# A state-space mixer's sample states: loads, multiplies and stores written in other places, the SiLUs queued behind an exponential, and the state stores issued from GpSimd's queue

## The chip, the cores and the metric

The kernel runs on one core of a Trainium2 chip. The metric is the device time of one execution in microseconds (us). The core has five engines with instruction queues of their own: TensorE (PE in the profile), VectorE (DVE), ScalarE (ACT), GpSimd (POOL) and SyncE (SP). Each queue runs in order; semaphores tie them together. SP computes nothing here and issues transfers (DMAs).

## The reference, cut to what matters

One inference step of a two-layer network for a prompt of 512 positions and 8 samples of 8 positions (64 more columns), with d_model 1024. Layer 0 is a convolution and attention mixer, layer 1 a Mamba-2 mixer with 32 heads of 64 channels, a state of 128 and 4 groups of 8 heads; each is followed by a convolutional feed-forward block. The change is in layer 1's mixer. What it computes for the 8 samples, whose states come in as `state_ssm` and go out as `ssm_s` (the prompt's last state goes out as `ssm_p`), is this:

```python
def step(hc, inp):                     # ssd_scan: the prompt in 4 chunks of 128, a sample in one of 8
    dec, st = inp
    return dec[..., None, None] * hc + st, hc
h_final, h_prev = lax.scan(step, h0, (chunk_decay, states))
y_off = jnp.einsum('bclgn,bcgrpn,bclgr->bclgrp', cc, h_prev, jnp.exp(acum))
y = (y_diag + y_off).reshape(b, t, h, p)
...
y = (y + d_skip[:, None] * xs).reshape(b, t, D_INNER) * jax.nn.silu(z)
y = rmsnorm(y.reshape(b, t, SSM_GROUPS, gs), gn_g).reshape(b, t, D_INNER)
return y @ w_out, new_conv, new_ssm
```

So each sample's old state is read by a product with C (`y_off`), multiplied by a decay, added to the sample's new part and stored.

## The kernel before, in words

All activations stay in the core's memory, channels in partitions, with 576 columns (512 prompt, 64 sample) taken in two halves of 288. A large projection is done as three matmuls for each 128 x 128 block of weights, because values are split in a high and a low part: lines 160, 161 and 162, tile `mm`, with `wh`/`wl` the weights' parts (made by ACT, line 150, and DVE, line 151) and `hh`/`hl` or `yh`/`yl` the activations'. These matmuls are most of the kernel's work.

The second mixer, `mix1`, goes over 4 groups g of 8 heads. `ssd(g)` is a Python generator that emits the group's scan in pieces; `run` puts pieces of projection work (the z projection of the group, `z_units`, and the output projection of the group before, `out_tile`) between them. `gate(g)` then multiplies by silu(z), normalises and splits the result. The Python order is not the order that runs: a scheduler, at build time, writes each engine's queue from it with the dependences and costs that it assumes. `keep_in_program_order(m)` makes the next matmul stay behind m on TensorE, and `issue_after(i)` makes what is written in it stay behind instruction i on i's engine.

Steps and names of `ssd(g)`:

- `hst` (lines 983 to 1000): the prompt's states at the ends of 4 chunks; the last is stored to `ssm_p` by SP (line 1000).
- `carried(t)` for t = 0..3: a load `ea2`, an exponential, the product `py` (line 1034).
- `decays(r)`, two for each t: SP loads `acb` (line 1017), ACT makes four ReLUs and an exponential of it (lines 1021, 1022), DVE multiplies it (line 1023).
- `outputs(t)`: eight matmuls `yp` (line 1047) that read the two `acb`; DVE adds them to `xs`.
- `samples(bh)`, after t = 1 and after t = 3: for four samples, SP loads their old states `h0` (line 1060; the profile cuts digits from names and calls it `h`), TensorE makes `pyo` from them (line 1064, four matmuls into four strips of 32 rows), DVE `yo` from it (line 1066), TensorE the new part `pst` (line 1071), GpSimd multiplies `h0` by the decay `cds` (line 1072), DVE adds `pst` (line 1075), SP stores it to `ssm_s` (line 1076).
- `ysp` (lines 1095, 1100): the samples' outputs, with a product that reads `yo`.

All of `xs`, `acb`, `h0`, `hst`, `zs`, `yh`/`yl` and others come from one list of 48 + 9 equal slots (`S`, `NSLOT`, `EXTRA`), first freed, first reused. A load into a slot waits until its last user is done, a store's landing included. GpSimd also sets and copies the borders of the convolution's buffers (`cbuf`, lines 789 to 798) for the next group's projections, and SP loads all weights.

Of the kernel before, what the change touches and what calls it, by code (L numbers as in the profile page):

```python
# [14 lines left out]
P = 128  # L15
NP = 512
# [34 lines left out]
class Builder:  # L51
    NSLOT = 48
    EXTRA = 9
# [721 lines left out]
    def mix1(self):  # L775
# [60 lines left out]
        v = self.Z("sp_v", W, bufs=1)  # L836
# [6 lines left out]
        e, z, z2, q = (self.Z(n_, W, bufs=1) for n_ in ("sp_e", "sp_z", "sp_z2", "sp_q"))  # L843
# [16 lines left out]
        nc.scalar.activation(ea, self.pv("alog", 0, 32), AF.Exp, bias=zero)  # L860
        da = self.Z("da", W, bufs=1)
# [52 lines left out]
        def ssd(g):  # L914
# [85 lines left out]
            nc.sync.dma_start(d["ssm_p"][g], H[3])  # L1000
# [13 lines left out]
            def decays(r):  # L1014

                acb = self.S("acb", NP)
                nc.sync.dma_start(acb, acd[8 * g + r, 0:NP].partition_broadcast(P))
                for c in range(4):
                    cs = slice(c * P, (c + 1) * P)
                    o = c * 32 + 8 * g + r  # L1020
                    nc.scalar.activation(acb[:, cs], acb[:, cs], AF.Relu, bias=ac[:, o:o + 1], scale=-1.0)  # L1021
                nc.scalar.activation(acb, acb, AF.Exp, scale=-1.0)
                nc.vector.tensor_tensor(acb, acb, cbm[:, :NP], op=MUL)
                return acb
# [14 lines left out]
            def outputs(t, ea2, pair):  # L1039

                yp = self.ps("yp", "yp")
                for c in range(4):
                    cs = slice(c * P, (c + 1) * P)
                    for hh in (1, 0):
                        r = 2 * t + hh
                        rows, ch = slice(hh * 64, hh * 64 + 64), slice(r * 64, r * 64 + 64)
                        m = nc.tensor.matmul(yp[rows, cs], xdt[c][:, ch], pair[hh][:, cs], start=True, stop=True)  # L1047
                        if c or not hh:
                            self.tc.keep_in_program_order(m)
                x = xs[t][:, :NP]  # L1050
                nc.vector.scalar_tensor_tensor(x, x, self.pv("dsk", 4 * g + t), yp, op0=MUL, op1=ADD)
                nc.vector.tensor_tensor(x[:, P:], x[:, P:], ea2, op=ADD)
                self.free(pair, ea2)

            def samples(bh):

                h0 = []
                for b4 in range(4):
                    h0.append(self.S("h0", NP))
                    nc.sync.dma_start(h0[-1], d["h0"][4 * bh + b4, g])  # L1060
                pyo = self.ps("pyo", "pyo")
                for b4 in range(4):
                    b = 4 * bh + b4
                    nc.tensor.matmul(pyo[b4 * 32:b4 * 32 + 32, :], cf[:, NP + 8 * b:NP + 8 * b + 32], h0[b4], start=True, stop=True)  # L1064
                o = self.S("yo", NP)
                nc.vector.tensor_tensor(hp(o), hp(pyo), eax[:, bh * 32 + 8 * g:bh * 32 + 8 * g + 8].unsqueeze(2).broadcast_to([P, 8, 64]), op=MUL)
                yo.append(o)
                for b4 in range(4):
                    b = 4 * bh + b4
                    pst = self.ps("pst")  # L1070
                    nc.tensor.matmul(pst, b3[bh][:, b4 * P:(b4 + 1) * P], x3[bh], start=True, stop=True)
                    nc.gpsimd.tensor_tensor(hp(h0[b4]), hp(h0[b4]),  # L1072
                                            cds[:, b * 32 + 8 * g:b * 32 + 8 * g + 8].unsqueeze(2).broadcast_to([P, 8, 64]),
                                            op=MUL)
                    nc.vector.tensor_tensor(h0[b4], h0[b4], pst, op=ADD)
                    nc.sync.dma_start(d["ssm_s"][b, g], h0[b4])
                    self.free(h0[b4])
                    if b4 % 2:
                        yield

            for t in range(4):
                ea2 = carried(t)
                pair = []
                for hh in range(2):
                    pair.append(decays(2 * t + hh))
                    yield
                outputs(t, ea2, pair)
                yield
                if t % 2:
                    yield from samples(t // 2)  # L1090
# [15 lines left out]
        def z_units(g):  # L1106
            zss[g] = [self.S("zs") for _ in range(4)]

            def evac(t):
                return lambda half, p: nc.scalar.activation(zss[g][t][:, HALF[half]], p[:, :HB], AF.Copy)  # L1110
            return [(d["w_in_o"][4 * g + t], P, evac(t)) for t in range(4)]

        def gate(g, yv):
# [4 lines left out]
            for t in range(4):  # L1118
                nc.scalar.activation(zs[t], zs[t], AF.Silu)
# [26 lines left out]
        for g in range(4):  # L1146
# [3 lines left out]
            if g:  # L1150
# [19 lines left out]
            if g:  # L1170
                self.free(prev)
# [180 lines left out]
```

## Time and profile before

| | |
|---|---|
| median of 3 runs | 1595.83 us (1595.36 to 1596.58) |
| the profiled execution | 1596.65 us, of which 1594.9 us is the span from the first to the last instruction |
| TensorE busy | 1560.2 us (98%) |
| VectorE, ScalarE, GpSimd busy | 999.7, 656.1, 149.4 us |
| mixer 1, from its norm to the start of the next block | about 676 to 1150 us of the span |

Times in the views are microseconds from the start of the span. A matmul's record gives its own duration, but TensorE is pipelined, so the next matmul starts before it ends: what a matmul costs on the path is the distance from its start to the next start. A row that groups matmuls counts records; one matmul with 512 columns of 32-bit data leaves two records (x2). In brackets behind a row stands how long the engine sat idle before it, and what ended that. "A <- B" in the list of waits reads: A waited for B.

### The profile page before, as it was taken

Reading aid. Unit: us, or ns where it says so; the run is one execution under the profiler, and the core shown is the slowest. Engines: PE = TensorE matmul, PEld = TensorE weight load, DVE = VectorE, ACT = ScalarE, POOL = GpSimd, SP = SyncE. Lnnn points to the kernel's source line nnn. Section 1 sums busy time; section 2 is a strip of 40 time slices with the busy share of each in tenths; the row PEclk is TensorE's granted clock in tenths of the full one; section 3 lists DMA queues with packets and bytes.
Section 4 is the critical chain, followed back from the end, with each engine's and each line's share of the span. In section 5 each row is a group of like instructions: output and inputs, shape, how many; then the busy total and the mean of one; then the engine's idle time right before and its main releaser. Section 6 shows DMA issues by size and latency. Waiting matters only on the chain.

```text
span 1594.9 us, 28738 instructions
## 1 busy us (share of the span) xinstructions
PE 1560.2 (98%) x11709; PEld 1479.2 (93%) x11709; DVE 999.7 (63%) x1750; ACT 656.1 (41%) x1210; POOL 149.4 (9%) x362
## 2 busy tenths in 40 slices
PE   8999999999999999999999999999999999999999
PEld 8976799999999999998987987998899999999999
DVE  7958486663564464678885686676776643663552
ACT  6257363321232222479654655556443221221220
POOL 0026001000000000101202101101110000000000
PEclk9999999999999999999999999999999999999999
DMA  7514223222222222226245226235222232223222
GB/s 229 117 54 102 70 83 101 80 81 92 80 77 84 93 80 75 74 82 203 74 120 186 74 81 195 89 96 182 81 89 84 80 91 83 80 73 97 83 82 76
DMA packets 69841, 157.60 MB, mean 99 GB/s; under 512 B 20158, under 2 KB 24510, under 8 KB 69710
## 3 DMA queue, kind: packets, MB, share of 16 engines
q1 hardware_dynamic: 69710, 155.77, 31.9%
q8 instruction: 92, 1.51, 0.4%
q14 instruction: 39, 0.32, 0.1%
HBM read 140.54 MB, written 15.21 MB: 98 GB/s over the span
## 4 chain that ended last, share of the span: by engine, by line
PE 82%; DVE 7%; ACT 4%; DMA 4%; issue 1%; POOL 1%; SPq 0%; ACTq 0%; DVEq 0%; POOLq 0%
PE mm L160 24%; PE mm L161 24%; PE mm L162 24%; DMA acb<-acd 2%; DVE cconv L801 1%; PE mm L559 1%; PE yp L1047 1%; DMA h<-in_h 1%; PE pyo L1064 1%; PE pt L182 1%; DVE ca L436 1%; ACT wh L150 1%; DVE wl L151 1%; ACT acb L1021 1%; PE pr L193 1%
## 5 line engine op out<-in xcount | busy, mean ns | idle before, releaser
L160 PE MATMUL mm<-hh,wh 128*128 128x288 f32 (+1 forms) x2288 | 682.8, 299 | 8.4 <-ACT wh L150 7.7
L161 PE MATMUL mm<-hl,wh 128*128 128x288 f32 (+1 forms) x2288 | 678.6, 297 | 0.0
L162 PE MATMUL mm<-hh,wl 128*128 128x288 f32 x2288 | 677.6, 296 | 0.0
L150 ACT ACTIVATE wh<-wr 128x1024 fp32r<-128x1024 f32 (+1 forms) x215 | 223.4, 1039 | 541.0 <-PE mm L161 273.6
L160 PEld LDWEIGHTS mm<-hh,wh 128*128 128x128 f32 (+1 forms) x2288 | 429.8, 188 | 14.9 <-ACT wh L150 7.9
L161 PEld LDWEIGHTS mm<-hl,wh 128*128 128x128 f32 (+1 forms) x2288 | 430.2, 188 | 5.6 <-issue 3.8
L162 PEld LDWEIGHTS mm<-hh,wl 128*128 128x128 f32 x2288 | 430.7, 188 | 2.7 <-issue 1.3
L151 DVE TENSOR_TENSOR wl<-wr,wh 128x1024 fp32r<-128x1024 f32 (+1 forms) x215 | 259.2, 1206 | 77.5 <-ACT wh L150 77.3
L160 PE MATMUL mm<-yh,wh 128*128 128x288 f32 x960 | 286.8, 300 | 2.2 <-ACT yh L170 2.2
L161 PE MATMUL mm<-yl,wh 128*128 128x288 f32 x960 | 288.2, 300 | 0.1
L162 PE MATMUL mm<-yh,wl 128*128 128x288 f32 x960 | 284.8, 297 | 1.4 <-DVE wl L151 1.4
L162 PEld LDWEIGHTS mm<-yh,wl 128*128 128x128 f32 x960 | 181.6, 189 | 6.1 <-issue 4.1
L161 PEld LDWEIGHTS mm<-yl,wh 128*128 128x128 f32 x960 | 181.9, 189 | 5.3 <-issue 4.0
L160 PEld LDWEIGHTS mm<-yh,wh 128*128 128x128 f32 x960 | 181.5, 189 | 4.4 <-ACT yh L170 2.6
L259 DVE TENSOR_TENSOR x<-x,mm 128x288 f32<-128x288 f32 x192 | 85.4, 450 | 157.4 <-PE mm L162 157.2
L304 DVE TENSOR_TENSOR gbuf<-mm,rs 128x224 f32<-128x224 f32 x44 | 17.2, 391 | 108.0 <-PE mm L162 108.0
L315 ACT ACTIVATE gsilu<-gconv,par 128x512 f32<-128x512 f32 x44 | 31.8, 723 | 115.5 <-DVE gconv L312 115.5
L312 DVE SCALAR_TENSOR_TENSOR gconv<-gbuf,par,gconv 128x592 f32<-128x592 f32 x88 | 73.1, 831 | 1.5
L325 DVE TENSOR_TENSOR gsilu<-mm,gsilu 128x288 f32<-128x288 f32 x88 | 40.0, 454 | 49.7 <-PE mm L162 49.7
L801 DVE SCALAR_TENSOR_TENSOR cconv<-cbuf,par,cconv 128x600 f32<-128x600 f32 x72 | 61.5, 857 | 13.0 <-ACT cconv L799 12.0
L307 POOL COPY fpo<-gbuf 128x2 f32<-128x2 f32 x44 | 12.4, 281 | 497.6 <-DVE gbuf L304 497.6
L1072 POOL TENSOR_TENSOR h<-h,cds 128x512 f32<-128x512 f32 x32 | 36.7, 1166 | 186.5 <-PE pyo L1064 167.8
(306 smaller groups left out, 1640.9 us busy)
## 6 DMA issues: line engine op xcount, KB each, us to landing
wr<-in_w_gate SPq DMA_DIRECT2D x44, 512.0 KB, 3.3
wr<-in_w_up SPq DMA_DIRECT2D x44, 512.0 KB, 3.3
wr<-in_w_in_o SPq DMA_DIRECT2D x40, 512.0 KB, 3.5
wr<-in_w_down SPq DMA_DIRECT2D x32, 448.0 KB, 3.4
wr<-in_w_down SPq DMA_DIRECT2D x16, 512.0 KB, 3.5
acb<-acd SPq DMA_DIRECT2D x32, 256.0 KB, 3.9
h<-in_h SPq DMA_DIRECT2D x32, 256.0 KB, 3.5
out_ssm_s<-h SPq DMA_DIRECT2D x32, 256.0 KB, 2.1
```

Source lines behind the costliest of these rows:

```text
L150: nc.scalar.activation(hi[:, :n], raw[:, :n], AF.Copy)
L151: nc.vector.tensor_tensor(lo[:, :n], raw[:, :n], hi[:, :n].bitcast(F32), op=SUB)
L160: nc.tensor.matmul(out, hi[:, ws], xh[:, sl], start=i == 0, stop=False)
L161: nc.tensor.matmul(out, hi[:, ws], xl[:, sl], start=False, stop=False)
L162: nc.tensor.matmul(out, lo[:, ws], xh[:, sl], start=False, stop=i == n - 1)
L259: nc.vector.tensor_tensor(self.x[m][:, sl], self.x[m][:, sl], p[:, :HB], op=ADD)
L304: nc.vector.tensor_tensor(g[:, 290:514], p[:, 0:224], rs[:, HB:NP], op=MUL)
L312: nc.vector.scalar_tensor_tensor(cv[:, :592], g[:, k:592 + k], w(k), cv[:, :592], op0=MUL, op1=ADD)
L315: nc.scalar.activation(sl[:, :NP], cv[:, :NP], AF.Silu, bias=b)
L325: nc.vector.tensor_tensor(sl[:, HALF[half]], p[:, :HB], sl[:, HALF[half]], op=MUL)
L801: nc.vector.scalar_tensor_tensor(cv[:, :600], g[:, k:600 + k], w(k), cv[:, :600], op0=MUL, op1=ADD)
L1072: nc.gpsimd.tensor_tensor(hp(h0[b4]), hp(h0[b4]), cds[:, b * 32 + 8 * g:b * 32 + 8 * g + 8].unsqueeze(2).broadcast_to([P, 8, 64]), op=MUL)
```

## The change

`samples(bh)` is cut in three. `load(bh)` issues the four `h0` loads: for bh = 0 before the first `carried`, for bh = 1 right behind the first `finish`. `begin(bh)`, called after `outputs` of t = 0 and t = 2, makes the four `pyo` matmuls (now from the fourth strip to the first, and kept in program order), the four GpSimd multiplies and `yo`. `finish(bh)`, called after `outputs` of t = 1 and t = 3, makes `pst` (placed behind the last `yp` matmul on TensorE), the addition and the store.

The stores to `ssm_p` and `ssm_s`, 4 and 32 of them, go from SP's queue to GpSimd's. In `gate` the four SiLUs are placed behind the group's last exponential on ACT. The list of slots grows from 48 + 9 to 48 + 11; five temporaries of softplus come from it instead of a pool of their own; `zs` is taken when it is first written; and `prev` (`yh`/`yl` of the group before) and, in the last group, `self.h` are freed as soon as they have been read.

```diff
-    EXTRA = 9
+    EXTRA = 11
...
-        v = self.Z("sp_v", W, bufs=1)
+        v = self.S("sp_v", W)
...
-            nc.sync.dma_start(d["ssm_p"][g], H[3])
+            nc.gpsimd.dma_start(d["ssm_p"][g], H[3])
...
-                nc.scalar.activation(acb, acb, AF.Exp, scale=-1.0)
+                self.last_exp = nc.scalar.activation(acb, acb, AF.Exp, scale=-1.0).ins
...
                 self.free(pair, ea2)
-
-            def samples(bh):
-
-                h0 = []
+                return m.ins
+
+            h0 = {}
+
+            def load(bh):
+                h0[bh] = []
                 for b4 in range(4):
-                    h0.append(self.S("h0", NP))
-                    nc.sync.dma_start(h0[-1], d["h0"][4 * bh + b4, g])
+                    h0[bh].append(self.S("h0", NP))
+                    nc.sync.dma_start(h0[bh][b4], d["h0"][4 * bh + b4, g])
+
+            def begin(bh):
+
                 pyo = self.ps("pyo", "pyo")
+                for b4 in (3, 2, 1, 0):
+                    b = 4 * bh + b4
+                    m = nc.tensor.matmul(pyo[b4 * 32:b4 * 32 + 32, :], cf[:, NP + 8 * b:NP + 8 * b + 32], h0[bh][b4],
+                                         start=True, stop=True)
+                    if b4 < 3:
+                        self.tc.keep_in_program_order(m)
                 for b4 in range(4):
                     b = 4 * bh + b4
-                    nc.tensor.matmul(pyo[b4 * 32:b4 * 32 + 32, :], cf[:, NP + 8 * b:NP + 8 * b + 32], h0[b4], start=True, stop=True)
+                    nc.gpsimd.tensor_tensor(hp(h0[bh][b4]), hp(h0[bh][b4]),
+                                            cds[:, b * 32 + 8 * g:b * 32 + 8 * g + 8].unsqueeze(2).broadcast_to([P, 8, 64]),
+                                            op=MUL)
                 o = self.S("yo", NP)
...
                 yo.append(o)
+
+            def finish(bh, behind):
+
                 for b4 in range(4):
                     b = 4 * bh + b4
                     pst = self.ps("pst")
-                    nc.tensor.matmul(pst, b3[bh][:, b4 * P:(b4 + 1) * P], x3[bh], start=True, stop=True)
-                    nc.gpsimd.tensor_tensor(hp(h0[b4]), hp(h0[b4]),
-                                            cds[:, b * 32 + 8 * g:b * 32 + 8 * g + 8].unsqueeze(2).broadcast_to([P, 8, 64]),
-                                            op=MUL)
-                    nc.vector.tensor_tensor(h0[b4], h0[b4], pst, op=ADD)
-                    nc.sync.dma_start(d["ssm_s"][b, g], h0[b4])
-                    self.free(h0[b4])
+                    with self.tc.issue_after(behind):
+                        nc.tensor.matmul(pst, b3[bh][:, b4 * P:(b4 + 1) * P], x3[bh], start=True, stop=True)
+                    nc.vector.tensor_tensor(h0[bh][b4], h0[bh][b4], pst, op=ADD)
+                    nc.gpsimd.dma_start(d["ssm_s"][b, g], h0[bh][b4])
+                    self.free(h0[bh][b4])
                     if b4 % 2:
                         yield

             for t in range(4):
+                if t == 0:
+                    load(0)
                 ea2 = carried(t)
...
-                outputs(t, ea2, pair)
+                last = outputs(t, ea2, pair)
                 yield
                 if t % 2:
-                    yield from samples(t // 2)
+                    yield from finish(t // 2, last)
+                    if t == 1:
+                        load(1)
+                else:
+                    begin(t // 2)
...
-            for t in range(4):
-                nc.scalar.activation(zs[t], zs[t], AF.Silu)
+            with self.tc.issue_after(self.last_exp):
+                for t in range(4):
+                    nc.scalar.activation(zs[t], zs[t], AF.Silu)
...
+                    if m == 7:
+                        self.free(prev)
                 ot = [lambda m=m: out_tile(m) for m in range(8)]
-                side = single(zu) + ot[:4] if g == 3 else ot + single(zu)
+
+                def last_h():
+                    self.free(self.h)
+                    self.h = []
+                side = single(zu) + [last_h] + ot[:4] if g == 3 else ot + single(zu)
```

Where the instructions then stand is shown at three places. The first is TensorE's queue in group 1. Before, around the first `samples` of that group; `h0_9242` to `h0_9248` are the four states:

```order
L1064 MATMUL pyo_9250<-h0_9242,cfm_7699 32x512
L1064 MATMUL pyo_9250<-h0_9244,cfm_7699 32x512
L1064 MATMUL pyo_9250<-h0_9246,cfm_7699 32x512
L1071 MATMUL pst_9262<-x3_8858,b3_8843 128x512
L160 MATMUL mm_9277<-yh_8441,wh_9210 128x288
...
L162 MATMUL mm_9277<-yh_8445,wl_9211 128x288
L1071 MATMUL pst_9267<-x3_8858,b3_8843 128x512
L160 MATMUL mm_9277<-yh_8447,wh_9210 128x288
L1064 MATMUL pyo_9250<-h0_9248,cfm_7699 32x512
L161 MATMUL mm_9277<-yl_8448,wh_9210 128x288
L162 MATMUL mm_9277<-yh_8447,wl_9211 128x288
```

Now, around `begin(0)` of the same group; `h0_9070` to `h0_9076` are the four states, and `acb_9204`, `acb_9196` are what `yp` of t = 1 reads:

```order
L991 MATMUL pst_9058<-xde_9056,btok_8822 128x512
L1035 MATMUL py_9082<-cfm_7695,hst_8978 128x128
...
L161 MATMUL mm_9148<-yl_8442,wh_9097 128x288
L1070 MATMUL pyo_9176<-h0_9076,cfm_7695 32x512
L1070 MATMUL pyo_9176<-h0_9074,cfm_7695 32x512
L1070 MATMUL pyo_9176<-h0_9072,cfm_7695 32x512
L1070 MATMUL pyo_9176<-h0_9070,cfm_7695 32x512
L1035 MATMUL py_9191<-cfm_7695,hst_8978 128x128
...
L1048 MATMUL yp_9212<-acb_9204,xdt_8916 64x128
L1048 MATMUL yp_9212<-acb_9196,xdt_8916 64x128
```

The four `pyo` matmuls stood in two pieces, the fourth behind two `pst` and ten other matmuls; now they stand together, and before `yp` of t = 0 and t = 1.

The second place is GpSimd's queue in the same group. Before:

```order
L797 COPY cso_7113<-cbuf_8777 128x24
L1072 TENSOR_TENSOR h0_9242<-h0_9242,cds_7372 128x512
L1072 TENSOR_TENSOR h0_9244<-h0_9244,cds_7372 128x512
L1072 TENSOR_TENSOR h0_9246<-h0_9246,cds_7372 128x512
L1072 TENSOR_TENSOR h0_9248<-h0_9248,cds_7372 128x512
L1072 TENSOR_TENSOR h0_9493<-h0_9493,cds_7372 128x512
```

Now:

```order
L797 COPY cso_7113<-cbuf_8777 128x24
L1076 TENSOR_TENSOR h0_9076<-h0_9076,cds_7372 128x512
L1001 DMA out_ssm_p<-hst_9060 128x512
L1076 TENSOR_TENSOR h0_9070<-h0_9070,cds_7372 128x512
L1076 TENSOR_TENSOR h0_9072<-h0_9072,cds_7372 128x512
L1076 TENSOR_TENSOR h0_9074<-h0_9074,cds_7372 128x512
L1091 DMA out_ssm_s<-h0_9070 128x512
L1091 DMA out_ssm_s<-h0_9072 128x512
L1091 DMA out_ssm_s<-h0_9074 128x512
L1091 DMA out_ssm_s<-h0_9076 128x512
L789 MEMSET cbuf_9789 128x3
L790 COPY cbuf_9789<-chist_7112 128x8x3
```

The store of `ssm_p` now stands behind the first multiply, which waits for `pyo`, and the four stores of `ssm_s` stand ahead of the border of a `cbuf`. On SP, `acb_9204` is loaded into the slot of `hst_9060`, which that store reads; before, too, one of the two `acb` of t = 1 was loaded into the stored `hst`'s slot.

The third place is TensorE's queue at the end of the mixer, where the output projection of group 3 begins. `yh_12285` and `yl_12286` to `yh_12291`, `yl_12292` are group 3's gated and split outputs, `yh_11038` to `yl_11045` group 2's, `pr` is the row of reciprocal norms for one half of the columns, and `mm_12540` is a tile of the second half. Before:

```order
L160 MATMUL mm_12483<-yh_11044,wh_12437 128x288
L193 MATMUL pr_12318<-dg_12319,ones_103 128x288
L161 MATMUL mm_12483<-yl_11045,wh_12437 128x288
L162 MATMUL mm_12483<-yh_11044,wl_12438 128x288
L160 MATMUL mm_12557<-yh_12285,wh_12519 128x288
L161 MATMUL mm_12557<-yl_12286,wh_12519 128x288
L162 MATMUL mm_12557<-yh_12285,wl_12520 128x288
L160 MATMUL mm_12557<-yh_12287,wh_12519 128x288
L161 MATMUL mm_12557<-yl_12288,wh_12519 128x288
```

Now:

```order
L160 MATMUL mm_12469<-yh_11044,wh_12437 128x288
L193 MATMUL pr_12356<-dg_12357,ones_103 128x288
L161 MATMUL mm_12469<-yl_11045,wh_12437 128x288
L162 MATMUL mm_12469<-yh_11044,wl_12438 128x288
L160 MATMUL mm_12483<-yh_11038,wh_12437 128x288
...
L161 MATMUL mm_12483<-yl_11045,wh_12437 128x288
L162 MATMUL mm_12483<-yh_11044,wl_12438 128x288
L160 MATMUL mm_12540<-yh_12285,wh_12519 128x288
L160 MATMUL mm_12576<-yh_12285,wh_12519 128x288
L161 MATMUL mm_12540<-yl_12286,wh_12519 128x288
L162 MATMUL mm_12540<-yh_12285,wl_12520 128x288
```

Before, two matmuls stood between the first half's `pr` and the first matmul that reads group 3's outputs; now fourteen that read group 2's stand between the second half's `pr` and it.

More of the change, by code (lines that the diff above doesn't have):

```diff
@@ L842, in mix1 @@
         nc.vector.tensor_tensor(v[0:64, 128:160], pt[0:64, 128:160], bias[0:64], op=ADD)
-        e, z, z2, q = (self.Z(n_, W, bufs=1) for n_ in ("sp_e", "sp_z", "sp_z2", "sp_q"))
+        e, z, z2, q = (self.S(n_, W) for n_ in ("sp_e", "sp_z", "sp_z2", "sp_q"))
         dt = self.Z("dt", W, bufs=1)
@@ L860, in mix1 @@
         nc.scalar.activation(ea, self.pv("alog", 0, 32), AF.Exp, bias=zero)
+        self.free(v, e, z, z2, q)
         da = self.Z("da", W, bufs=1)
@@ L1106, in z_units, with go @@
         def z_units(g):
-            zss[g] = [self.S("zs") for _ in range(4)]
+            zss[g] = []
             def evac(t):
-                return lambda half, p: nc.scalar.activation(zss[g][t][:, HALF[half]], p[:, :HB], AF.Copy)
+                def go(half, p):
+                    if half == 0:
+                        zss[g].append(self.S("zs"))
+                    nc.scalar.activation(zss[g][t][:, HALF[half]], p[:, :HB], AF.Copy)
+                return go
             return [(d["w_in_o"][4 * g + t], P, evac(t)) for t in range(4)]
@@ L1169, in mix1 @@
                     f()
-            if g:
-                self.free(prev)
             if g < 3:
```

## The prediction

> **What bounds the kernel now.** I read the page first, its span, its busy times and the engine line of the chain that ended last:
>
> ```profile
> span 1594.9 us, 28738 instructions
> PE 1560.2 (98%) x11709; PEld 1479.2 (93%) x11709; DVE 999.7 (63%) x1750; ACT 656.1 (41%) x1210; POOL 149.4 (9%) x362
> PE 82%; DVE 7%; ACT 4%; DMA 4%; issue 1%; POOL 1%; SPq 0%; ACTq 0%; DVEq 0%; POOLq 0%
> ```
>
> TensorE is the bound: 98% busy. A gain can come from its idle time, from matmuls that occupy it longer than they need to, or from its clock. The windows view (length, then busy time with instruction counts of PE, PEld, DVE, ACT and POOL, then the granted clock) says how much of that lies in the mixer:
>
> ```profile
> 676.00:1150.00 474.00, 456.36 (x3346) 411.14 (x3345) 345.96 (x585) 288.83 (x594) 69.07 (x126) 0.99 0.39 124
> 716.00:756.00 40.00, 39.02 (x299) 34.47 (x298) 34.25 (x55) 37.42 (x73) 5.86 (x10) 1.00 0.69 208
> 1136.00:1138.00 2.00, 0.12 (x1) 0.00 (x0) 2.00 (x6) 2.00 (x5) 0.00 (x0) 1.00 0.03 8
> 1140.00:1146.00 6.00, 6.00 (x28) 6.00 (x28) 3.69 (x9) 1.46 (x5) 0.00 (x0) 0.50 0.25 87
> ```
>
> So 474.0 - 456.4 = 17.6 us idle in the mixer. After an empty stretch at 1136 us, a stretch runs at a clock of 0.50. In group 0 (716 to 756) ACT is busy 37.4 of 40 us and TensorE still 39.0, so even there ACT's load hardly reaches TensorE. Third, the list of TensorE's waits in the mixer (total, times, longest):
>
> ```profile
> PE yp L1047 <- DVE acb L1023: 5.6, 7, 1.3
> PE pyo L1064 <- DMA h<-in_h: 3.4, 3, 1.7
> PE mm L160 <- ACT yh L170: 2.2, 1, 2.2
> PE ysp L1095 <- DVE yo L1066: 1.6, 1, 1.6
> PE mm L162 <- DVE wl L151: 1.4, 1, 1.4
> PE pst L1071 <- DVE ea L1036: 0.8, 1, 0.8
> PE pst L1071 <- DVE h L1075: 0.8, 2, 0.5
> ```
>
> Fourth, the matmuls that the change moves: their group, and TensorE's timeline around them.
>
> ```profile
> L1064 PE MATMUL pyo<-h,cfm 128*32 128x512 f32 x64 | 18.9, 605 | 3.5 <-DMA h<-in_h 3.4
> ```
>
> ```profile
> 741.89 1.06 PE L1064 MATMUL pyo<-h,cfm 128*32 128x512 f32 x8
> 742.89 0.73 PE L1071 MATMUL pst<-x,b 96*128 96x512 f32 x2
> 743.46 0.29 PE L160 MATMUL mm<-hh,wh 128*128 128x288 f32 x1
> 743.59 0.29 PE L161 MATMUL mm<-hl,wh 128*128 128x288 f32 x1
> ...
> 840.55 1.06 PE L1064 MATMUL pyo<-h,cfm 128*32 128x512 f32 x6
> 841.54 0.50 PE L1071 MATMUL pst<-x,b 96*128 96x512 f32 x1
> ...
> 844.07 1.04 PE L1064 MATMUL pyo<-h,cfm 128*32 128x512 f32 x2
> 845.05 0.40 PE L161 MATMUL mm<-yl,wh 128*128 128x288 f32 x1
> ...
> 1126.34 1.04 PE L1064 MATMUL pyo<-h,cfm 128*32 128x512 f32 x2
> ```
>
> Here lies the busy time that need not be. Four `pyo` matmuls together (x8) hold TensorE from 741.89 to 742.89, 1.00 us. Three (x6) take 0.99 us, and one alone (x2) takes 844.07 to 845.05, 0.98 us. The four write four different strips of 32 rows and run beside one another; one alone costs the same. From the first of these rows to the last the 32 matmuls come in 18 pieces, where 8 would do.
>
> **The change part by part.**
>
> *`pyo` kept together.* In the changed order all eight groups of four stand without anything between. Ten pieces of about 0.98 us go: 9.8 us, all on TensorE and so on the path. The matmuls that stood between the pieces run as before (743.46 to 743.59: 0.13 us each).
>
> *`yp` not split.* Three `yp` groups are split before and whole after. What a split costs:
>
> ```profile
> 834.96 0.43 PE L1047 MATMUL yp<-acb,xdt 128*64 128x128 f32 x2
> 835.32 0.40 PE L160 MATMUL mm<-yh,wh 128*128 128x288 f32 x1
> ```
>
> 0.36 us each, 1.1 us together.
>
> *Loads of `h0` early.* They are now issued a `t` and more ahead of their `pyo`, from free slots. The 3.4 us that `pyo` waits for them go. If one load comes late, the whole group waits, since it is kept in order (a rival below).
>
> *`pst` and `yo`.* The multiplies on GpSimd come right after `pyo`, a `t` before their additions, and `yo` long before `ysp`: the waits of `pst` (0.8 + 0.8) and of `ysp` (1.6) go, 3.2 us. Nothing else is late there: `pst` still needs DVE's additions of the pair before it, which now wait for no GpSimd work.
>
> *SiLUs and table loads.* With the SiLUs behind the exponentials, ACT's order has 13 table loads fewer (49 to 36) of this kind:
>
> ```profile
> 821.72 1.28 ACT L1031 ACT_TABLE_LOAD   x1 [2.98 <-DMA ea<-acd]
> ```
>
> 13 x 1.28 = 16.7 us of ACT's time. By the window at 716 us I put it at nothing on TensorE: ACT has slack in all groups but the first, and there TensorE waits about 1 us in 40. Its cover is the projection matmuls; without them it could give up to the 5.6 us of `yp`'s waits.
>
> *The end of the mixer.*
>
> ```profile
> 1135.19 0.67 PE L193 MATMUL pr<-dg,ones 96*128 96x288 f32 x2
> ...
> 1138.34 0.40 PE L160 MATMUL mm<-yh,wh 128*128 128x288 f32 x1 [2.22 <-ACT yh L170]
> ...
> 1139.74 0.43 PE L161 MATMUL mm<-yl,wh 128*128 128x288 f32 x1
> 1139.97 0.45 PE L162 MATMUL mm<-yh,wl 128*128 128x288 f32 x1
> ...
> 1146.50 0.33 PE L161 MATMUL mm<-yl,wh 128*128 128x288 f32 x1
> ```
>
> From `pr` to the first matmul that reads its result is 3.15 us (1135.19 to 1138.34). Now fourteen matmuls stand between, 14 x 0.13 = 1.8 us, and `pr` itself takes 0.3: the wait becomes about 1.0 us, of 2.2. Put 1.0 us of gain, not 1.2. The clock: from 1139.74 to 1146.50, 6.8 us, the clock is at half (a matmul costs 0.23, 1139.74 to 1139.97, and more, in place of 0.13), so 3.4 us are lost. It follows the longest gap in the mixer; none of the waits of up to 1.7 us has such a stretch behind it. I count 3.4 us of gain. The Trainium skill, TensorE: Matmul & The Clock Gate, Part 1, says that the clock is set by how busy the array was over windows of 3.4 us that run freely; by that rule, and the rows agree, a 1.0 us gap would mostly keep full speed, but the phase decides, and the sum would be the same with a chance in it.
>
> Gains: 9.8 + 1.1 + 3.4 + 3.2 + 1.0 + 3.4 = 21.9 us.
>
> *The stores on GpSimd's queue.* No transfer of that kind is in this trace.
>
> ```profile
> L1072 POOL TENSOR_TENSOR h<-h,cds 128x512 f32<-128x512 f32 x32 | 36.7, 1166 | 186.5 <-PE pyo L1064 167.8
> ...
> acb<-acd SPq DMA_DIRECT2D x32, 256.0 KB, 3.9
> ...
> out_ssm_s<-h SPq DMA_DIRECT2D x32, 256.0 KB, 2.1
> ```
>
> ```profile
> SPq L1076 <- DVE h L1075: 46.3, 24, 7.1
> ```
>
> SP waited 46.3 us for the additions ahead of these stores, with later loads queued behind it; now they don't queue there, and that is in the terms above. GpSimd holds each instead. For the issue I take 1.0 us, near a GpSimd multiply over the same bytes (1.17), with SP's 0.4 as the lower bound; for the landing 2.1 to 4.1 us, the fastest and slowest that SP's stores of this size show (2.1 above, 4.05 below). 36 issues are 36 us on an engine that is busy 69 of 474: capacity is no limit, but delay is. Behind the stores stand borders of `cbuf`, due many matmuls later, and on SP nine loads of `acb` into slots of stored tiles.
>
> The tightest is group 1's `acb` for t = 1. Before, in the chain and on the timeline:
>
> ```profile
> 825.57 4.05 DMA out_ssm_p<-hst
> 829.64 5.31 DMA acb<-acd
> ```
>
> ```profile
> 822.70 1.02 PE L990 MATMUL pst<-xde,btok 128*128 128x512 f32 x2
> ...
> 837.76 0.77 PE L1047 MATMUL yp<-acb,xdt 128*64 128x128 f32 x10 [0.58 <-DVE acb L1023]
> ```
>
> Counted from T, the start of the last `pst` (822.70), `yp` ran at T + 15.1: 2.9 to the store, 4.05, 5.3, and 2.8 of ACT and DVE. Now TensorE is there sooner. Its work from T is 0.9 for `pst`, 48 matmuls of 0.13 (6.3), two `py` of 0.76, `pyo` 1.0 and a `yp` group 1.0: T + 10.7. The store stands behind a multiply that waits for `pyo`: `pyo` ends at T + 3.4, the multiply at T + 4.6, the issue at T + 5.6, landing at T + 7.7 to 9.7, `acb` (3.9, the median, to 5.3) at T + 11.6 to 15.0, and 2.8 more: T + 14.4 to 17.8. `yp` waits 3.7 to 7.1 us, against 0.6. I take 4.0, near the quicker end, because the loads of `h0` no longer share the time. By the same counting the other `yp` waits come to about 3 us (0.7 in group 0, 0.3 in group 2, 1.0 in group 3, 1.0 in the rest). So 7.0 replaces 5.6: a loss of 1.4. A 4 us gap is longer than the one at 1136, so a slow clock behind it has an even chance: 1.7. For waits that a new order brings and that I can't name I take off 3.0, twice the one of `wl` in the list.
>
> The Trainium skill, DMA: Bandwidth & Descriptors, section Issuing engines are not separate DMA queues, says that another issuing engine saves only the sequencer's time to initiate. By that rule the move would be worth 36 x 0.4 = 14 us of SP, which is off the path, thus nothing; the row of 46.3 us speaks of a queue that stood still, which is more.
>
> The sum: 21.9 - 1.4 - 1.7 - 3.0 = 15.8. Against the profiled execution (1594.9 of span and 1.75 around it, 1596.65 in all, 0.8 above the median) that is 1580.8; from the median, **1580.0 us**.
>
> **The rivals.**
>
> *The new waits cost more.* The `acb` of t = 1 wait for `ssm_p` in groups 1 to 3 alike, 4 us each, and two of them bring a slow stretch: 12 us of `yp` waits for 5.6, and 6.8 of clock, from 21.9 leaves 8.7: 1587. For it: the slots are taken in the order in which they are freed, and every group runs the same code. Against: in groups 2 and 3 the store stands ahead of the multiplies.
>
> *Nearly all waits go.* With ACT's 16.7 us, `yp` waits fall to 4 us, nothing new comes: 21.9 + 1.6 = 23.5, 1572.3. The ceiling is 17.6 of idle, 3.4 of clock and 10.9 of pieces, 32 us: 1564.
>
> *Slower: GpSimd's stores land late.* Nine `acb` loads wait for such a store, in about six places. If a store lands from 5 us on instead of 2.1, each place has a gap of over 2.2 us and, as at 1136, a slow stretch behind it: 6 x (2.2 + 3.4) = 33.6 from 21.9: 1607.5. That decides from about 4 us per place. For it: four stores stand in a row there, with DVE busy 73% beside them. Against: the binding ones are 256 KB like SP's of 2.1 us, and the slots have a `t` of slack. The Trainium skill, SBUF — State Buffer, under The "DVE blocks DMA" trap, says that DVE's two-port operations keep GpSimd from writing the descriptors of its own transfers, and gives one that took 3.1 us in place of 0.6; DVE's rows here are tensor_tensor, which it doesn't count among them. No run here shows it.
>
> *It doesn't do what it says.* The `h0` loads land late and a kept-together `pyo` waits for its last one. At today's longest wait (1.7) in all eight groups, 13.6 in place of 3.4, 3.4 of the gain and 10.2 more are gone: 15.8 - 13.6 = 2.2, 1593.6.
>
> **How the numbers follow.** The forecast 0.52, the costlier waits 0.22, nearly all gone 0.14, late stores 0.07, late loads 0.05. The range leaves out the last two and some of the tails: 1569 to 1591; it takes in 1587 and 1572.3, and a wait of 7.1 with the clock's 3.4. A measurement can tell about 0.2%, 3.2 us, from no change. Faster by more than that: the first three, less a little, 0.87; within it 0.05; slower 0.08.
>
> **What would show it.** In the new profile: `pyo` in 8 pieces, all x8, with no wait on its loads; `ysp` and `pst` without waits; no stretch of half clock after the mixer; in group 1 a `yp` wait of some 4 us on `acb`, the only long one, ended by a load behind `ssm_p`. The forecast is wrong if `pyo` still comes in pieces or waits, if `yp` waits sum to over 12 us, if stores from GpSimd land later than about 5 us, or if TensorE shows a new wait outside these lines.

## The result and the profile after

| | before | changed |
|---|---|---|
| median of 6 runs, us | 1595.59 (1592.40 to 1596.58) | 1586.24 (1583.07 to 1591.16) |
| ratio, 95% interval | | 0.9947 (0.9928 to 0.9966) |
| span of the profiled execution, us | 1594.9 | 1584.8 |

The change gains 9.4 us by the medians; 15.8 were forecast, with a range of 1569 to 1591. The page of the changed kernel, its span, busy times and the kinds of transfer (queue, packets, MB, share of 16 engines):

```profile
span 1584.8 us, 28679 instructions
PE 1549.6 (98%) x11709; PEld 1479.6 (93%) x11709; DVE 998.2 (63%) x1750; ACT 642.0 (41%) x1197; POOL 171.5 (11%) x398
q0 software_dynamic: 2880, 9.44, 1.5%
```

TensorE's busy time fell by 10.6 us (1560.2 to 1549.6), close to the 10.9 that were forecast for the pieces of `pyo` and `yp`; both busy times contain stretches at half clock, 11.4 us of them before and 13.7 now. The idle time did not fall in this execution: 1594.9 - 1560.2 = 34.7 before, 1584.8 - 1549.6 = 35.2 now. ACT lost 13 instructions and 14 us, and GpSimd gained 36 transfers, which show as a queue of a new kind.

TensorE's waits in the mixer (total, times, longest), against the list of before:

```profile
PE yp L1048 <- DVE acb L1024: 8.8, 4, 3.8
PE pst L1089 <- DVE h L1090: 3.3, 4, 1.1
PE pst L1089 <- DVE ea L1037: 1.5, 1, 1.5
PE mm L162 <- DVE wl L151: 1.3, 2, 0.9
```

`pyo`'s wait for its loads (3.4), `ysp`'s for `yo` (1.6) and the 2.2 at the mixer's end are gone, as forecast. In their place `yp` waits 3.2 us more and `pst` 3.2 us more (8.8 for 5.6, and 4.8 for 1.6). The group of `pyo` by lines (it was 18.9 us busy and waited 3.5):

```profile
L1070 PE MATMUL pyo<-h,cfm 128*32 128x512 f32 x64 | 8.5, 605 | 0.0
```

All eight groups are x8. Now TensorE's timeline in group 1, around the longest wait:

```profile
828.31 1.02 PE L991 MATMUL pst<-xde,btok 128*128 128x512 f32 x2
...
830.72 1.06 PE L1070 MATMUL pyo<-h,cfm 128*32 128x512 f32 x8
...
840.36 0.29 PE L162 MATMUL mm<-yh,wl 128*128 128x288 f32 x1
844.48 1.98 PE L1048 MATMUL yp<-acb,xdt 128*64 128x128 f32 x16 [3.82 <-DVE acb L1024]
846.38 0.61 PE L160 MATMUL mm<-yh,wh 128*128 128x288 f32 x1
846.78 0.45 PE L161 MATMUL mm<-yl,wh 128*128 128x288 f32 x1
```

This is the wait that was forecast at 4 us. With T = 828.31, the start of the last `pst`, `yp` starts at T + 16.2, inside the forecast T + 14.4 to 17.8. The even chance of a slow clock behind it went against the kernel: `yp` takes 1.98 us in place of 1.09. What ended it, on GpSimd, SP and ACT:

```profile
831.91 2.54 POOL L1076 TENSOR_TENSOR h<-h,cds 128x512 f32<-128x512 f32 x1 [23.45 <-PE pyo L1070]
834.40 0.58 POOL L1001 DMA_DIRECT2D out_ssm_p<-hst  x1
```

```profile
837.03 0.32 SPq L1018 DMA_DIRECT2D acb<-acd  x1
```

```profile
841.76 1.28 ACT L1022 ACTIVATE acb<-acb,ac 128x128 f32<-128x128 f32 x4 [6.79 <-DMA acb<-acd]
```

The store of `ssm_p` stands behind the multiply and goes out at T + 6.1; `acb` is loaded once it has landed, at T + 8.7. The chain is the one of the prediction, link by link; the multiply took 2.5 us in place of the 1.2 that were put for it, the issue 0.6 in place of 1.0. The next wait in the list, 1.6 us at 965.24, also goes back to a load behind `ssm_p`, issued at 957.38 when that store had landed. And here is what SP waited for, of the state stores, before:

```profile
SPq L1017 <- DMA out_ssm_p<-hst: 9.3, 3, 4.6
SPq L1030 <- DMA out_ssm_s<-h: 1.1, 2, 0.6
SPq L1017 <- DMA out_ssm_s<-h: 0.9, 1, 0.9
```

and after:

```profile
SPq L1031 <- DMA out_ssm_s<-h: 12.5, 2, 8.4
SPq L1018 <- DMA out_ssm_p<-hst: 11.2, 2, 6.8
...
SPq L1018 <- DMA out_ssm_s<-h: 3.1, 2, 2.5
SPq L1063 <- DMA out_ssm_p<-hst: 1.2, 1, 1.2
```

SP no longer waits for additions to store what they made, but it waits 28.0 us for landings, 11.3 before, with later loads queued behind. Whether this is what cost the rest was the question for the experiments.

### The profile page after: what moved, and what is told of

The parts are those of the page before. It is cut to its first block, busy times and chain, and to the rows that moved or that the text cites. A ratio compares the mean times of both kernels' runs of the same rounds, so it can differ in the third digit from the quotient of the medians.

```text
span 1584.8 us, 28679 instructions
## 1 busy us (share of the span) xinstructions
PE 1549.6 (98%) x11709; PEld 1479.6 (93%) x11709; DVE 998.2 (63%) x1750; ACT 642.0 (41%) x1197; POOL 171.5 (11%) x398
## 5 line engine op out<-in xcount | busy, mean ns | idle before, releaser
L1022 ACT ACTIVATE acb<-acb,ac 128x128 f32<-128x128 f32 x128 | 41.2, 390 | 60.8 <-DMA acb<-acd 43.5
```

## Experiments

The kernels were timed in three groups of four (e1 to e4, e5 to e8, e9 to e12), each group on one chip with runs of the kernel before beside it. Differences in us are between medians; ratios are to the kernel before. Kernels of different groups are compared by their distance from it.

**e1, the changed kernel again.**

> The changed kernel once more, as the mark for the three beside it. Both theories: 1586 us (1583 to 1589), 8 pyo pieces, a yp wait of 3 to 5 us in group 1 with a half-clock stretch behind it, the sum of the yp waits 8 to 10 us.

1583.56 us, ratio 0.9936 (0.9919 to 0.9953), 9.9 us below the kernel before. Its profiled execution has `yp` waits of 6.5 us in all, the longest 3.3, less than the 8 to 10 us expected, and 8 pieces of `pyo`. The shortfall against 15.8 is there again. Its idle time is 28.8 us, where the first profile of the same kernel had 35.2, so a few us of idle time differ from one execution to the next.

**e2, one dependency taken away.**

```diff
-            self.free(H.pop(), btok)
+            self.free(btok, H.pop())
```

> The slot of btok is given back before that of the stored hst, so that the acb of t = 1 in groups 1 and 2 no longer waits for the store of ssm_p and an h0 load, due later, does; TensorE's order is the same row for row. Theory A (the shortfall sits in that one dependency): group 1's yp wait falls from 3.8 to at most 1.0, no half clock behind it, one of group 2's 1.5 us waits goes too: 4 to 6 us less than the changed kernel, about 1581. Theory B (the acb loads are late for other reasons, crowded transfers and a busy ACT, and a wait taken away comes back at the next load): at most 1 us less.

1578.07 us, ratio 0.9899 (0.9883 to 0.9916): 5.5 us below e1, as theory A had it, with TensorE's order the same. The wait at t = 1 in group 1 is gone, but not everything with it; TensorE's timeline there, now with a wait at t = 2 and one of `pst`:

```profile
843.32 0.50 PE L1089 MATMUL pst<-x,b 96*128 96x512 f32 x1 [1.48 <-DVE h L1090]
...
851.62 1.09 PE L1048 MATMUL yp<-acb,xdt 128*64 128x128 f32 x16 [2.13 <-DVE acb L1024]
```

**e3, only the four `ssm_p` stores back on SP.**

```diff
-            nc.gpsimd.dma_start(d["ssm_p"][g], H[3])
+            nc.sync.dma_start(d["ssm_p"][g], H[3])
```

> Only the four ssm_p stores go back to SP's queue; the 32 ssm_s stores stay on GpSimd's. Theory A: the store goes out at about T + 3 instead of T + 6 and acb follows 3 us sooner: group 1's yp wait falls from 3.8 to 1 us or less, 3 to 5 us less than the changed kernel. Theory B: at most 1 us less. If GpSimd's stores as such were what costs (theory C), 4 of 36 going back would give at most 1 us as well.

1582.42 us, ratio 0.9932 (0.9917 to 0.9947): 1.1 us below e1, which no interval tells from nothing, and at the edge of what theories B and C allowed. The wait at t = 1 did shrink as theory A said, but 14 us later `yp` waits 2.1 us, and in half clock:

```profile
838.19 1.09 PE L1048 MATMUL yp<-acb,xdt 128*64 128x128 f32 x16 [0.75 <-DVE acb L1024]
...
852.40 1.84 PE L1048 MATMUL yp<-acb,xdt 128*64 128x128 f32 x16 [2.12 <-DVE acb L1024]
```

So theory A, one dependency, was too narrow: the next wait took over. It is as long in e2 (2.13 us), where no half clock follows it; the last section shows why, and the table at the end of this one how much of e2's 5.5 us is clock.

**e4, `pyo` in halves.** The first two of each four stay in `begin`, the other two are issued behind the next t's `py`:

```diff
+                with self.tc.issue_after(self.last_py):
+                    strips(bh, (1, 0))
```

> Each group of four pyo matmuls is cut into two and two, with the three py matmuls of the next t between them (in one group, more); nothing is taken away or added. If a piece costs about 0.98 us whatever it holds, 8 pieces more are 7.8 us more than the changed kernel (6 to 10, GpSimd's multiplies being a little later too). If a matmul costs its share (0.25 us each), nothing changes: within 1.5 us.

1584.91 us, ratio 0.9946 (0.9931 to 0.9962): 1.4 us above e1, and neither expectation. The page of e1 and that of e4:

```profile
span 1579.9 us, 28679 instructions
PE 1551.1 (98%) x11709; PEld 1480.4 (94%) x11709; DVE 1000.9 (63%) x1750; ACT 642.9 (41%) x1197; POOL 172.5 (11%) x398
```

```profile
span 1582.2 us, 28680 instructions
PE 1555.6 (98%) x11709; PEld 1479.2 (93%) x11709; DVE 1000.1 (63%) x1750; ACT 641.8 (41%) x1197; POOL 173.5 (11%) x398
```

Each of the 16 pieces takes 0.98 us on the timeline, so the price of a piece was right. Busy time rose by 4.5 us beside e1, in which 6.8 us more ran at half clock, and by 6.0 beside the first profile of the changed kernel; idle time fell, to 26.6 us from 28.8 and 35.2. So against e1 some 8 us more of matmuls at full clock met 3.4 us less lost to half clock and 2.2 us less idle time; what TensorE spends on pieces, it in part no longer spends waiting.

**e5, all 36 stores back on SP.**

```diff
-                    nc.gpsimd.dma_start(d["ssm_s"][b, g], h0[bh][b4])
+                    nc.sync.dma_start(d["ssm_s"][b, g], h0[bh][b4])
```

(and `ssm_p` as in e3)

> All 36 state stores back on SP's queue, the rest of the change kept. Theory A (the stores' move is worth little by itself, the ssm_p store apart): within 2 us of the changed kernel (1584 in the run before this one, ratio about 0.994), with h0 and acb loads queued behind SP's waits for additions (46 us of them before) and yp waits of 6 to 9 us. Theory C (GpSimd's stores cost): 3 us or more less than the changed kernel. Theory E (the move is what frees the loads): 4 us or more above it, with pyo waiting for h0 again.

1576.87 us, ratio 0.9897 (0.9883 to 0.9911), 16.1 below the kernel before; the changed kernel stood 9.4 and 9.9 below. Theory C: with the stores' move the kernel is 6 to 7 us slower. What SP waits for, here:

```profile
SPq L1018 <- DMA out_ssm_p<-hst: 8.8, 2, 5.4
SPq L1031 <- DMA out_ssm_s<-h: 2.6, 2, 1.6
```

With the two smaller rows of 0.9 and 0.4, SP's waits for landings are 12.7 us in place of 28.0. It waits 41 us for additions again, and `pyo` doesn't wait for a load, so theory E is wrong: the early issue frees the loads, not the other queue. The longest `yp` wait, 2.4 us at 841.02, still goes back to a load behind `ssm_p`. TensorE's order differs from the changed kernel's in places, since the scheduler weighs the stores otherwise, so e5 alone doesn't settle it.

**e6, the stores' move alone, on the kernel before.** The edits of e3 and e5 the other way round.

> The kernel before with only its 36 state stores moved to GpSimd's queue; samples, SiLUs and slots as before. Theory A: within 2 us of the kernel before. Theory E: 3 us or more faster, SP's waits for additions gone and pyo's 3.4 us wait for h0 with them. Theory C: 3 us or more slower.

1600.60 us, ratio 1.0041 (1.0028 to 1.0054): 7.7 us slower, theory C again. Here too TensorE's order differs in places from that of the kernel it is compared with. SP's waits, where 2.0 us for `out_ssm_s` stood before:

```profile
SPq L1017 <- DMA out_ssm_s<-h: 19.4, 8, 5.7
SPq L1017 <- DMA out_ssm_p<-hst: 10.7, 3, 5.6
SPq L1060 <- DMA out_ssm_s<-h: 4.6, 3, 2.6
```

With a fourth row of 3.3, its waits for landings are 38.0 us in place of 11.3. And who pays, on TensorE's timeline:

```profile
858.99 1.09 PE L1047 MATMUL yp<-acb,xdt 128*64 128x128 f32 x16 [2.60 <-DVE acb L1023]
...
985.82 1.43 PE L1047 MATMUL yp<-acb,xdt 128*64 128x128 f32 x16 [3.42 <-DVE acb L1023]
...
1114.32 1.09 PE L1047 MATMUL yp<-acb,xdt 128*64 128x128 f32 x16 [2.69 <-DVE acb L1023]
```

The second and the third of these waits go back to an `acb` load that SP could issue only when an `ssm_s` store had landed (at 975.68 and 1103.88); the first goes back to a load that waited for an instruction of VectorE. The `yp` waits rise from 5.6 to 9.4 us and the half clock in the mixer from 6.8 to 17.1 us (five stretches).

**e7, the multiplies on DVE.** On e2, `nc.gpsimd.tensor_tensor` in `begin` becomes `nc.vector.tensor_tensor`.

> As e2 (btok's slot first), and the 32 multiplies by the decay go from GpSimd to DVE, 32 x 0.68 = 22 us more for DVE. Theory F (GpSimd's multiplies and DVE's products of acb hold each other up: in e2 one took 3.60 us in place of 0.68 beside three multiplies, and yp waits for it): DVE rows of 1 us and more for acb vanish, group 1's yp wait falls from 2.1 to under 1, 1 to 4 us less than e2. Rival: DVE is 73% busy there and the longer queue delays acb just as much: within 1 us of e2, or up to 6 us more.

1579.46 us, ratio 0.9916 (0.9902 to 0.9930); beside e2's 0.9899 no gain. The slow products of `acb` are gone, and `yp` waits 5.0 us in place of 5.3, the longest 2.2. The two engines do hold each other up (last section), but that is not what bounds the time; the rival was right.

**e8, SiLUs free.** The `issue_after(self.last_exp)` in `gate` is taken away.

> The SiLUs are no longer placed behind the last exponential, the rest of the change kept; in group 1 the scheduler then cuts pyo in two and two. My reckoning (ACT's table loads are hidden): 13 or so table loads more, within 2 us of the changed kernel. Rival: ACT's loads of 1.28 us stand in the chain from acb to yp: 4 to 8 us more, in the yp waits.

1582.15 us, ratio 0.9920 (0.9904 to 0.9936), not to be told from the changed kernel, though the 13 table loads are back (49 in all) and `pyo` comes in nine pieces. ACT's table loads are hidden, as reckoned.

**e9, e2 and e5 together.**

> e2 and e5 together: btok's slot back first, and all 36 state stores on SP's queue. If the two edits shorten different waits (e2 group 1's acb behind ssm_p; e5 the slots of the stored h0), the time is 3 us or more below each, about 1573 and a ratio of 0.987. If both shorten the same chain of slot, load, ACT, DVE and yp, the second gives nothing: a ratio of 0.989 to 0.991, within 2 us of each.

1572.61 us, ratio 0.9862 (0.9844 to 0.9880): 20.8 us below the kernel before, and the best version. The two edits add up (5.5 and 6 to 7 on top of 9.9), so they shorten different waits: where e5 still waits 2.4 us behind `ssm_p`, the same `yp` waits 0.5 here. Its list of waits and its page:

```profile
PE yp L1048 <- DVE acb L1024: 3.2, 4, 1.9
PE pst L1089 <- DVE ea L1037: 1.7, 1, 1.7
PE pst L1089 <- DVE h L1090: 1.0, 1, 1.0
```

```profile
span 1570.3 us, 28674 instructions
PE 1544.3 (98%) x11709; PEld 1475.6 (94%) x11709; DVE 999.7 (64%) x1750; ACT 644.5 (41%) x1199; POOL 149.0 (9%) x362
```

Idle time is 26.0 us, in e5 28.3 (1575.2 - 1546.9).

**e10, e2 and e3 together.**

> e2 and e3 together: btok's slot back first, ssm_p alone back on SP's queue, ssm_s still on GpSimd's. If what ssm_p does to the slots is all gone with e2, this equals e2: ratio 0.989 to 0.991. If GpSimd's place of the ssm_p store hurts in another way too (an h0 load now waits for it), 2 us or more below e2.

1579.67 us, ratio 0.9907 (0.9890 to 0.9924): equal to e2. After e2 the queue of the `ssm_p` store no longer matters; what e9 gains beyond it, 7.1 us, comes from moving the 32 `ssm_s` stores, the order that the scheduler then writes included.

**e11, each new state stored twice.** Behind the store of `ssm_s`, GpSimd stores the same tile to a scratch tensor as well.

> The changed kernel with a second store of each of the 32 new states, to a scratch in DRAM, on GpSimd's queue behind the first: each slot comes free later, by about 0.6 us of issue and a share of the transfer, and GpSimd issues 32 more. Theory C (a later end of GpSimd's stores delays the loads that wait for their slots): 4 us or more above the changed kernel, in the yp waits and the half-clock stretches behind them, above all at t = 2 and t = 3. Rival (the loss of the move lies in the one ssm_p wait and in the order, not in the ssm_s stores): within 2 us.

1590.45 us, ratio 0.9976 (0.9963 to 0.9989): 3.0 below the kernel before, so by the medians 6 to 7 us above the changed kernel and by the ratios 5 to 6: theory C. TensorE's order is that of the changed kernel, so here its order is no rival; ACT has 38 table loads in place of 36. The second stores also move 8 MB more and hold GpSimd 0.54 us each, which this run doesn't separate from the later landing. In its profiled execution, the fastest of its runs, the stores land after a median of 3.7 us:

```profile
out_ssm_s<-h POOLq DMA_DIRECT2D x32, 256.0 KB, 3.7
```

One `yp` wait that the changed kernel doesn't have, 1.9 us at 991.73, goes back to an `acb` load that was issued at 982.55, when a second store had landed; a SiLU and two table loads on ACT stand between that load and `yp`.

**e12, `pyo` in halves with all stores on SP.**

> e4's pyo in halves (17 pieces here), with all state stores on SP's queue as in e5. In e4, 7 us more of busy TensorE cost only 1.4, since waits shrank by as much. If TensorE's waits swallow a piece's price wherever a chain of loads ends just after it, they do so less here, where fewer waits are left: 3 to 6 us above e5. If pieces cost their full price outside such waits: 8.8 us above e5.

1579.51 us, ratio 0.9903 (0.9883 to 0.9923): by the medians 2.6 above e5 and by the ratios 1, below both expectations.

```profile
span 1576.4 us, 28672 instructions
PE 1553.7 (99%) x11709; PEld 1476.1 (94%) x11709; DVE 998.6 (63%) x1750; ACT 641.7 (41%) x1197; POOL 151.3 (10%) x362
```

Idle time is 22.7 us, 5.6 less than in e5, where busy time is 6.8 us less. With 17 pieces of `pyo`, one less than before the change, this kernel is 13.9 us faster than the one before. What it has is the rest of the change: the loads issued early and the multiplies made early, the new end of the mixer, `yp` in one piece.

**The share of half clock.** Each run's span and mean granted clock are on record. Span times (1 - clock) is an estimate of what half clock took from a run, and span times clock of what is left, since matmuls take about twice as long in such a stretch (`yp` above 1.98 us in place of 1.09). Means in us; the clock has three digits, which is up to 0.8 us in a single run:

| | runs | at full clock | lost to half clock |
|---|---|---|---|
| before, beside e1 to e4 | 10 | 1584.5 | 7.0 |
| before, beside e5 to e8 | 11 | 1585.3 | 6.7 |
| before, beside e9 to e12 | 17 | 1585.3 | 6.9 |
| the changed kernel, first runs | 6 | 1576.3 | 8.5 |
| e1, the changed kernel | 6 | 1575.2 | 6.6 |
| e2, `btok` first | 5 | 1572.4 | 3.5 |
| e3, `ssm_p` on SP | 6 | 1574.5 | 6.3 |
| e4, `pyo` in halves | 6 | 1577.9 | 5.5 |
| e5, stores on SP | 4 | 1571.3 | 4.3 |
| e6, only the stores moved | 5 | 1587.4 | 11.2 |
| e7, multiplies on DVE | 5 | 1575.0 | 3.8 |
| e8, SiLUs free | 6 | 1575.6 | 4.2 |
| e9, e2 and e5 | 4 | 1565.6 | 4.7 |
| e10, e2 and e3 | 4 | 1570.7 | 6.7 |
| e11, stored twice | 12 | 1578.6 | 9.8 |
| e12, halves, stores on SP | 5 | 1572.3 | 4.4 |

The change's gain is almost all work and waits, not clock. Of e2's gain over e1 about half is clock, and of e6's loss more than half. The pieces put back cost 2.7 us at full clock in e4 and 1.0 in e12, far less than 7.8 and 8.8.

## Why the prediction was right or wrong

The sign and the range were right, 1586.2 in 1569 to 1591, and most of what was to disappear did. The size was not: 9.4 of 15.8. Several terms were mis-sized in opposite directions, so it is partly luck that the sum came as near as it did. Term by term:

- *`pyo` in 8 pieces of 1.0 us, `yp` whole: 10.9 us of busy time.* Measured 10.6, half clock included. (Two `yp` groups were split by other matmuls, at 834.96 and 959.63, not three, so the term itself was 10.5.) The step that failed is the half-sentence "all on TensorE and so on the path". Putting back 8 of the 10 pieces cost 1.4 us (e4) and, with the stores on SP, putting back 9 cost 1 to 2.6 (e12), not 7.8 and 8.8. In these profiles `yp` or `pst` waits just behind such places for a chain of slot, load, ACT and DVE; idle time fell as busy time rose (e12), so much of a saved microsecond of work comes back as a wait.
- *`pyo`'s loads, `yo`, the end of the mixer.* The 3.4 and 1.6 are gone. The end's wait fell from 2.2 to 0.2, better than 1.0, and its 6.8 us of half clock went.
- *`pst`: 1.6 us of waits to go.* They rose to 4.8 (2.9 in e1), in places where TensorE now comes early. "Nothing else is late there" was wrong: `pst` waits for DVE's additions, through the two banks that it shares with `py`, and DVE is as busy as before (998.2 us of 999.7).
- *Group 1's `acb` behind `ssm_p`: 4 us and an even chance of half clock.* Right in place and chain and nearly in size: 3.8, then 3.3 in e1, and half clock both times. The price in the end is less clear. e2 took the wait away and gained 5.5 us, of which some 3 are clock by the estimate above; e3 cut the same wait to 0.75 and gained 1.1.
- *Half clock: 3.4 to be gained at the end of the mixer, 1.7 to be lost.* The stretch at the end went, but others came: over the runs, 7.0 us were lost before and 6.6 in e1 (8.5 in the first runs). A stretch was priced at the 6.8 us that the one before lasted; most last 3.4 and cost 1.7.
- *The other stores: nothing but 0.3 to 1.0 us a place.* Wrong. The move of the stores as a whole costs 6 to 7 us (e5) or 7.7 (e6), that of the `ssm_s` stores 7.1 (e9 beside e10), and doubling these alone costs 5 to 7 more (e11). An `ssm_s` store lands after 2.7 us (median) in place of 2.1, and is issued 0.30 us behind its addition in place of 0.03; the slowest took 8.0 in place of 4.6. (The prediction took SP's 2.1 for the fastest landing; it is the median.) The rival "GpSimd's stores land late" had the direction, but was put at 5 us of landing and beyond.
- *SiLUs: nothing.* Right (e8).
- *3.0 us for waits that I couldn't name.* The idle time was forecast to fall by 3.2 net. In the first profiled execution it rose by 0.5, in e1's it was 5.9 lower, so one profile doesn't size this term. In the first one two more stretches at half clock lie outside the mixer (at 165 and 196 us, where TensorE's order is unchanged); they cost it 3.4 us that the change has no part in.

Without the stores' move the change gives 16.1 us (e5). That this is the 15.8 of the forecast is chance: the sum took too much for the pieces and too little for the stores' queue.

What was shown: the move of the stores costs 6 to 7 us (e5, e6, e9 beside e10), a second store of the same buffers costs 5 to 7 with TensorE's order unchanged (e11), and the two parts add up (e9). What stays open: by which waits the `ssm_s` stores cost the changed kernel these microseconds. In e6 and e11 some `yp` waits go back to such a landing. In the changed kernel's own profile none does: two go back to `ssm_p` (3.8 and 1.6 us) and two to loads that waited for an instruction of VectorE (1.5 and 1.9). Nor does the total that SP waits for landings tell the time: it is 28.0 us in the changed kernel, but 29.1 in e2, which is 5.5 us faster than e1.

## What to carry to other kernels

A store into DRAM is a link of a chain when its buffer is reused by a load: price its queue by when it lands and by who waits for the buffer, not by whether the queue is free. Where an engine that is 98% busy waits for chains of loads, time saved on it just ahead of such a wait is not a gain; test it by putting the work back. And look at the order in which buffers are given back: swapping two names in one `free` was worth 5.5 us beside the 9.9 of the whole change. Before a difference of a few microseconds is put down to a wait, see how much of it is half clock.

## What the runs showed of the hardware

- *GpSimd and DVE hold each other up.* In e2 GpSimd's multiplies (both inputs in the core's memory) fell on DVE's products of `acb` (the same). DVE's timeline and GpSimd's:

```profile
828.85 0.68 DVE L1024 TENSOR_TENSOR acb<-acb,cbm 128x512 f32<-128x512 f32 x1
...
830.99 4.20 DVE L1024 TENSOR_TENSOR acb<-acb,cbm 128x512 f32<-128x512 f32 x2
```

```profile
827.39 3.04 POOL L1076 TENSOR_TENSOR h<-h,cds 128x512 f32<-128x512 f32 x1 [23.43 <-PE pyo L1070]
830.38 0.58 POOL L1001 DMA_DIRECT2D out_ssm_p<-hst  x1
830.98 3.05 POOL L1076 TENSOR_TENSOR h<-h,cds 128x512 f32<-128x512 f32 x3
```

  Two products take 4.2 us in place of 1.4 while three multiplies run at their usual 1.0 each, and the multiply at 827.39 takes 3.0 in place of 1.0 beside DVE instructions that keep their usual length (0.68 for `acb`). In e7, with no multiply on GpSimd, no product took over 0.7. The Trainium skill, SBUF — State Buffer, section Who interferes with whom, says that a DVE instruction with two inputs in SBUF contends with a GpSimd instruction that reads SBUF; this trace agrees.

- *Half clock comes in pieces of 3.4 us, and depends on how a gap falls into them.* In the profiled executions every stretch of half clock that isn't cut off by the end of the span lasts 3.41 or 6.83 us. Within one execution the stretches start whole multiples of 3.413 us apart (in the first profile of the changed kernel 3, 12 and 202 of them), so a span can be cut into windows along them. The prediction took half clock to follow only the longest gap. In these profiles it goes mostly with the idle time inside one window. The same wait in group 1 in e2 (2.13 us) and in e3 (2.12 us), in the windows view (length, then busy time with counts of PE, PEld, DVE, ACT and POOL, then the granted clock and two figures on transfers), e2 first:

```profile
849.81:853.22 3.41, 1.60 (x20) 1.46 (x21) 1.67 (x2) 2.24 (x6) 0.00 (x0) 1.00 0.26 98
853.22:856.64 3.42, 3.42 (x27) 3.32 (x25) 1.91 (x3) 0.92 (x3) 0.00 (x0) 1.00 0.78 242
```

```profile
849.18:852.59 3.41, 1.29 (x13) 1.08 (x13) 1.83 (x2) 2.14 (x5) 0.00 (x0) 1.00 0.52 207
852.59:856.01 3.42, 3.42 (x23) 3.09 (x21) 1.82 (x3) 1.50 (x4) 0.00 (x0) 0.50 0.57 119
```

  In e2 the wait lies across two windows, 1.81 us of it in the later one, and full clock goes on; in e3 it lies in one window whole, and the next window runs at half clock. In all 14 profiles, from 120 us of the span on, each of the 26 windows at full clock with 1.9 us or more idle was followed by one at half clock, five of 14 with 1.5 to 1.9 us, and 6 of 3623 with less. (Idle time is not all of it: before the stretch at 196 us TensorE's records leave no gap.) This is part of why one kernel's runs spread (1583 to 1591 for the changed one, at mean clocks of 0.997 to 0.991). The Trainium skill, TensorE: Matmul & The Clock Gate, Part 1, gives windows of 3.4 us that run freely, and the lengths and distances agree; it lets the clock drop after an idle window, and here 1.9 us of idle in one was enough.

- *A store from GpSimd's queue* of 256 KB holds GpSimd for 0.54 to 0.75 us and, for `ssm_s`, lands after 2.7 us (median), against 2.1 from SP in the kernel before; the prediction had put its issue at 1.0.
